# Stick-breaking attention inside a hybrid decoder layer: the float32 work of two heads put side by side

## The chip, the core and the metric

The kernel runs on one core of one Trainium2 chip. The metric is the device time of one execution in microseconds (us), the median of three runs. Lower is better.

## The reference, cut to what matters

The program is one decoder layer: an RMS norm, one input projection into q, k, v (8 heads of 128) and into the channels of a short convolution, stick-breaking attention, the convolution, an output projection and a SwiGLU block. The change concerns the attention alone. For each head, with 528 positions (16 meta tokens and 512 of the sequence) and 128-wide blocks of keys:

```python
z = einsum('bqhd,bkhd->bhqk', q_blk, k_ctx) / sqrt(HEAD_DIM)
causal = kpos[None, :] < qpos[:, None]
log_beta = log_sigmoid(z)
log_keep = where(causal, log_sigmoid(-z), 0.0)
log_pass = cumsum(log_keep, axis=3, reverse=True) - log_keep
w = where(causal, exp(log_beta + log_pass), 0.0)
o = einsum('bhqk,bkhd->bqhd', w, v_ctx)
```

Here z are the logits, w the weights and o the head's output.

## The kernel before

Activations lie transposed: the partitions are channels (or keys), the free dimension is the position. Large products are made of float32r matmuls on values split in two, a high part and a low part (`split`: a cast on ScalarE, a subtraction on VectorE), three matmuls for each pair of tiles. Weights are loaded in pieces of 512 KB, split likewise (lines 203 and 206), and prepared two pieces ahead of the matmuls that use them.

`head(h)` runs three input products for a head, k (`pk`), q (`pq`) and v (`pv`), each over 16 tiles of the contraction ("k tiles"), so 48 k tiles a head. TensorE is kept busy by these products. Attention is cut into steps and put between the k tiles by a counter: `after(n, work)` puts work behind n more k tiles, `tick()` counts each k tile down and runs what is due. A head's attention thus lies in the time of the next head's three products.

Counted from the end of head h's v product (heads 1 to 7), the steps stand like this:

- k tile 6: `turned` turns v with five transposes (lines 626 and 627, float32, into the PSUM tiles `va` and `vb`); VectorE and ScalarE then make `vh`, `vl` and `v32` of it. `attend` follows in the same place. Its logits `z` are in three parts, one for each key block 2, 1, 0 (lines 650 to 652, float32r); the last two key blocks have their own small float32 matmuls, which write the columns 272 to 432 of `z` 2 (lines 648 and 649, "the last logits").
- behind the logits: ScalarE and VectorE make the log terms (lines 673 to 693), with GpSimd for the causal zeros.
- k tile 20 (14 behind `attend`): the running sums of part 2 (`sums`, lines 700 to 703); part 1 six k tiles later, part 0 another six.
- k tile 43 (11 behind part 0): `mix`, the output `o` of 512 columns. Key blocks 0 to 2 are float32r (lines 735 to 737). The last two key blocks are float32: line 738 with 144 columns and line 739 with 16. Then `o` is read by ScalarE (742, and 378 for its squares) and VectorE (743, 379), its stage tile `st_o` is stored (745), and `mix_x(h)` is put behind 742 on ScalarE and behind 743 on VectorE. `mix_x` combines blocks of the input for the convolution (lines 532 to 541): four instructions on ScalarE, six on VectorE, two DMAs.

Head 0 has other counts: transposes at 15, `attend` at 21, sums at 30, 36 and 42, `mix` at 53, which is k tile 5 of the stretch in which head 1's transposes stand at 6. In the same 48 k tiles the next head's own norms are made: `qk_norm` of k puts its sums of squares (lines 555 and 556) 8 k tiles behind the k product, that of q 9 behind the q product.

The pool `sm` has four PSUM tiles of one bank, shared by `va`, `vb`, `z`, `c` (the running sums), `ss_...` (the norms) and `o`. `stage` has two tiles under the tag `st_o`, used by `st_o` and by the two `st_x` of `mix_x`. The order of each engine's queue is laid down before the run by a planner: program order is the priority, `issue_after` forces an order on one engine, `high_priority` lifts an instruction.

After head 7 come the convolution's products. Their inputs are partly read back from DRAM on GpSimd's queue: `mixed` (line 820) and new columns of `n` (line 879).

Of the kernel before, what the change touches and what calls it, by code (L numbers as in the profile page):

```python
# [9 lines left out]
F32 = mybir.dt.float32  # L10
F32R = mybir.dt.float32r
AF = mybir.ActivationFunctionType
ALU = mybir.AluOpType
PSUM = bass.MemoryType.PSUM

P = 128
D = 2048
SEQ = 512
META = 16
L = META + SEQ  # L20
# [6 lines left out]
T2 = SEQ // 2  # L27
EPS = 1e-6

Q0 = [0, 112, 240, 368, 496]  # L30
# [3 lines left out]
def hybrid_layer(ctx: ExitStack, tc: tile.TileContext, xT, w_in, w_out, w_gu, w_down, vecs, out):  # L34
# [10 lines left out]
    ve, sc, gp, pe = nc.vector, nc.scalar, nc.gpsimd, nc.tensor  # L45
# [16 lines left out]
    def t512(cols=SEQ, tag="t", bufs=6):  # L62
        n_tmp[0] += 1
        return tmp.tile([P, cols], F32, tag=tag, bufs=bufs, name=f"tmp{n_tmp[0]}")

    def small(name):
        return sm.tile([P, 512], F32, tag="sm", name=name)
# [6 lines left out]
    g_att, g_cnv = vec[:, 32:40], vec[:, 40:48]  # L74
# [244 lines left out]
    def after(k_tiles, work):  # L319
        waiting.append([k_tiles, work])  # L320
# [33 lines left out]
    def product(parts, acts):  # L354
        for _ in product_steps(parts, acts, len(acts)):
            pass

    def split(hi, lo, src, eng=ve):
        return sc.copy(hi, src), eng.tensor_tensor(lo, src, hi.bitcast(F32), ALU.subtract)  # L359
# [13 lines left out]
    def square_sum(acc, src, first, s=None, eng=gp):  # L373
        if first:
            sc.activation(acc, src, AF.Square)
        else:
            s = t512(src.shape[-1], "r", 3)[:, : src.shape[-1]] if s is None else s
            sc.activation(s, src, AF.Square)
            eng.tensor_tensor(acc, acc, s, ALU.add)
# [56 lines left out]
    def side_by_side(ps):  # L436
        return [(ps[:, 0, :], 0, T2), (ps[:, 1, : L - T2], T2, L)]

    def add_up(ps):
        low = t512(L, "r", 3)[:, :T2]  # L440
        sc.copy(low, ps[:, 0, :T2])
        ve.tensor_tensor(ps[:, 0, T2:], ps[:, 0, T2:], low, ALU.add)

    def two(t):
        return t.rearrange("p (a b) -> p a b", a=2)

    def read_qk(ps, g, cols):

        raw = t512(L, "e", 2)[:, :cols]
        s = t512(L, "e2", 2)[:, :cols]  # L450
        sc.activation(s, ps, AF.Square)
        last = sc.activation(raw, ps, AF.Copy, scale=g)
        return raw, s, cols, last
# [34 lines left out]
    v32 = apool.tile([P, 256], F32, name="v32")  # L488
# [6 lines left out]
    acc_a = accp.tile([P, SEQ], F32, name="acc_a")  # L495
# [19 lines left out]
    oa_dram = [dram.tile([P, 2, SEQ], F32R, name=f"oa_dram{h}") for h in range(HEADS)]  # L515

    def stage(name):
        return stpool.tile([P, 4 * N], F32R, tag="st_o", bufs=2, name=name)
# [9 lines left out]
    def mix_x(k):  # L528

        x = xs[k]  # L530
        for i in range(2):
            sc.activation(x[:, 2 * i : 2 * i + 2], x[:, 2 * i : 2 * i + 2], AF.Copy, scale=g_mix[:, k + 8 * i : k + 8 * i + 1])
        a0, a1, b0, b1 = (x[:, m] for m in range(4))
        ve.tensor_tensor(b1, b1, a1, ALU.subtract)
        ve.tensor_tensor(a1, a0, a1, ALU.subtract)
        ve.scalar_tensor_tensor(a0, b1, -1.0, a0, ALU.mult, ALU.subtract)
        ve.scalar_tensor_tensor(b0, a0, -1.0, b0, ALU.mult, ALU.subtract)
        for m in (2, 0):
            st = stage(f"st_x{k}_{m}").rearrange("p (a b n) -> p a b n", a=2, b=2)
            split(st[:, :, 0], st[:, :, 1], x[:, m : m + 2])  # L540
            gp.dma_start(mix_dram[k // 4][:, 2 - m : 4 - m, k % 4], st.rearrange("p a b n -> p a (b n)"))
# [38 lines left out]
    def head(h):  # L580

        if h:
            pk = pp.tile([P, 2, 512], F32, tag="pp", name=f"pk{h}")
            product(side_by_side(pk), n_hl)
            add_up(pk)
        with tc.issue_after(split_q0[0].ins) if h == 1 else nullcontext():
            read = read_qk(flat(pk), g_k, L) if h else read_k0
        kn = kns[0]
        kh, kl = lent["kh"], lent["kl"]
        after(8 if h else 4, qk_norm(read, kn[:, :L], (kh, kl, 384), f"k{h}"))  # L590

        if h:
            load_mix(h - 1)
            pq = pp.tile([P, 2, 512], F32, tag="pp", name=f"pq{h}")
            product([(pq[:, 0, :], META, L)], n_hl)
        read = read_qk(pq[:, 0, :], gq_s, SEQ) if h else read_q0
        qn, qh, ql = read[0], lent["qh"], lent["ql"]
        after(9 if h else 7, qk_norm(read, None, (qh, ql, SEQ), f"q{h}", ("sh", "sl") if h else ("qh", "ql")))

        pv = pv0  # L600
        if h:
            pv = pp.tile([P, 2, 512], F32, tag="pp", name=f"pv{h}")
            product(side_by_side(pv), n_hl)
            add_up(pv)
        vts = []

        def scale_v():
            vts.append(t512(L, "e", 2) if h else stpool.tile([P, 4 * N], F32, tag="st_o", bufs=2, name="v0"))
            with tc.high_priority(0 if h else 1 << 20):
                ve.tensor_tensor(vts[0][:, :L], flat(pv), r, ALU.mult)  # L610

        if h:
            scale_v()
        else:
            after(2, scale_v)
        if h:
            after(6, lambda: attend(h, kn, kh, kl, qn, qh, ql, turned(h, vts[0])))
        else:
            after(15, lambda: vts.append(turned(h, vts[0])))
            after(21, lambda: attend(h, kn, kh, kl, qn, qh, ql, vts[1]))  # L620

    def turned(h, vt):

        ta, tb = small(f"va{h}"), small(f"vb{h}")
        for b in range(4):
            pe.transpose(ta[:, b * P : (b + 1) * P], vt[:, b * P : (b + 1) * P], ident)
        pe.transpose(tb[:16, :P], vt[:, 512:L], ident)
        vh = apool.tile([P, 384], F32R, tag="vh", name=f"vh{h}")
        vl = apool.tile([P, 384], F32R, tag="vl", name=f"vl{h}")
        with nullcontext() if h else tc.issue_after(split_q0[1].ins):  # L630
            split(vh, vl, ta[:, :384])
            ve.tensor_copy(v32[:16, P:], tb[:16, :P])
            last = ve.tensor_copy(v32[:, :P], ta[:, 384:512])
        if not h:
            behind[0] = last
        return vh, vl

    def attend(h, kn, kh, kl, qn, qh, ql, v):

        vh, vl = v  # L640

        zs = {}
        for b in (2, 1, 0):
            zs[b] = z = small(f"z{h}_{b}")
            kk, q0 = slice(b * P, (b + 1) * P), Q0[b]
            n = SEQ - q0
            if b == 2:
                pe.matmul(z[:, 272:416], kn[:, 384:512], qn[:, 368:], start=True, stop=True)
                pe.matmul(z[:, 416:432], kn[:, 512:640], qn[:, 496:], start=True, stop=True)
            pe.matmul(z[:, :n], kh[:, kk], qh[:, q0:], start=True, stop=False)  # L650
            pe.matmul(z[:, :n], kh[:, kk], ql[:, q0:], start=False, stop=False)
            pe.matmul(z[:, :n], kl[:, kk], qh[:, q0:], start=False, stop=True)


        lw = apool.tile([P, 1344], F32, tag="lw", name=f"lw{h}")
# [14 lines left out]
        for s in (2, 1, 0):  # L670
            a, b = SEG[s]
            z = zs[s][:, : b - a]
# [57 lines left out]
        def mix(ws):  # L730
            o = small(f"o{h}")
            for b in range(3):
                kk, q0 = slice(b * P, (b + 1) * P), Q0[b]
                th, tl = ws[b]
                pe.matmul(o[:, q0:], vh[:, kk], th, start=b == 0, stop=False)
                pe.matmul(o[:, q0:], vh[:, kk], tl, start=False, stop=False)
                pe.matmul(o[:, q0:], vl[:, kk], th, start=False, stop=False)
            pe.matmul(o[:, Q0[3] :], v32[:, :P], lw[:, 1184:1328], start=False, stop=False)
            pe.matmul(o[:, Q0[4] :], v32[:, P:], lw[:, 1328:1344], start=False, stop=True)
            g = g_att[:, h : h + 1]  # L740
            st = stage(f"st_o{h}")[:, : 2 * SEQ].rearrange("p (a b) -> p a b", a=2)
            hi = sc.activation(st[:, 0], o, AF.Copy, scale=g)
            lo = ve.scalar_tensor_tensor(st[:, 1], o, g, st[:, 0].bitcast(F32), ALU.mult, ALU.subtract)
            square_sum(acc_a, o, h == 0, eng=ve)
            gp.dma_start(oa_dram[h], st)
            if h < HEADS - 1:
                with tc.issue_after(hi.ins), tc.issue_after(lo.ins):
                    mix_x(h)

        after(14 if h else 9, lambda: sums(2))  # L750

    for h in range(HEADS):
        head(h)
# [345 lines left out]
    for i, j in enumerate(OUT_TILES):  # L1099
# [83 lines left out]
        else:  # L1183
# [8 lines left out]
            st = two(wide_tmp("st", F32R, 2))  # L1192
# [264 lines left out]
```

## Time and profile before

| what | value |
|---|---|
| time, median of 3 runs | 2020.65 us (2020.52 to 2020.66) |
| profiled execution: its own time | 2020.05 us |
| profiled execution: span, first to last instruction | 2018.3 us |
| TensorE busy | 2013.5 us |
| VectorE / ScalarE / GpSimd busy | 1729.9 / 1080.7 / 337.4 us |

The profile shows one execution. Its own time is 1.75 us more than its span, and 0.6 us less than the median of the runs. Busy time of TensorE is the time in which some matmul was under way; a matmul's record overlaps the next one's, so the distance from start to start tells what one costs.

### The profile page before, as it was taken

The numbers are of one execution on the slowest core, as the hardware profiler recorded it, in microseconds if no ns is written. First come the engines' busy times: TensorE is split into PE (matmuls) and PEld (weight loads), VectorE is DVE, ScalarE is ACT, GpSimd is POOL, SyncE is SP. The second block draws the span as 40 slices with busy tenths as digits, with TensorE's granted clock in tenths as the row PEclk, the third lists the DMA queues.
The fourth block names the chain that finished last, engine by engine and source line by source line (L and its number), as shares of the span: only waits on it lengthen the run. The fifth ranks groups of instructions, "written<-read, shape, count | busy, mean of one in ns | idle before, by whom it ended". The sixth has DMA issues, their size and how long they took to land.

```text
span 2018.3 us, 39281 instructions
## 1 busy us (share of the span) xinstructions
PE 2013.5 (100%) x15934; PEld 1949.8 (97%) x15934; DVE 1729.9 (86%) x2215; ACT 1080.7 (54%) x1574; POOL 337.4 (17%) x508
## 2 busy tenths in 40 slices
PE   9999999999999999999999999999999999999999
PEld 9989999999998889999999999999999999999999
DVE  7887778698888779999998898988988978888888
ACT  7876777354454435555555555555555554444443
POOL 0111111200014430111110110110110333131211
PEclk9999999999999999999999999999999999999999
DMA  6333344823256555565554544554554999797864
GB/s 223 119 133 116 127 140 133 295 95 116 99 203 189 161 155 197 163 176 174 178 155 149 178 152 151 176 155 143 176 160 144 297 342 352 166 324 190 222 150 90
DMA packets 156662, 356.44 MB, mean 177 GB/s; under 512 B 13696, under 2 KB 68224, under 8 KB 155712
## 3 DMA queue, kind: packets, MB, share of 16 engines
q1 hardware_dynamic: 72640, 216.76, 32.6%
q0 software_dynamic: 83696, 137.12, 25.0%
q8 instruction: 125, 2.05, 0.4%
q14 instruction: 57, 0.47, 0.1%
q10 hardware_dynamic: 144, 0.04, 0.0%
HBM read 275.88 MB, written 77.99 MB: 175 GB/s over the span
## 4 chain that ended last, share of the span: by engine, by line
PE 100%; DVE 0%; issue 0%
PE x L909 14%; PE x L913 14%; PE x L912 14%; PE z L909 7%; PE z L912 7%; PE z L913 7%; PE y L909 3%; PE y L912 3%; PE y L913 3%; PE pq L348 3%; PE pk L348 2%; PE pv L348 2%; PE pq L346 1%; PE pv L341 1%; PE pk L341 1%; PE pk L346 1%
## 5 line engine op out<-in xcount | busy, mean ns | idle before, releaser
L203 ACT CAST sw_split<-sw_in 128x1024 fp32r<-128x1024 f32 (+3 forms) x671 | 662.1, 989 | 695.1 <-PE x L912 172.3
L206 DVE TENSOR_TENSOR sw_split<-sw_in,sw_split 128x1024 fp32r<-128x1024 f32 (+3 forms) x671 | 778.0, 1160 | 136.7 <-ACT sw_split L203 128.6
L913 PE MATMUL x<-f,sw_split 128*128 128x256 f32 x1400 | 385.1, 275 | 0.0
L909 PE MATMUL x<-f,sw_split 128*128 128x256 f32 x1400 | 385.1, 275 | 0.0
L912 PE MATMUL x<-f,sw_split 128*128 128x256 f32 x1400 | 385.0, 275 | 0.0
L913 PEld LDWEIGHTS x<-f,sw_split 128*128 128x128 f32 x1400 | 262.8, 188 | 0.2 <-DVE sw_split L206 0.2
L912 PEld LDWEIGHTS x<-f,sw_split 128*128 128x128 f32 x1400 | 262.8, 188 | 0.0
L909 PEld LDWEIGHTS x<-f,sw_split 128*128 128x128 f32 x1400 | 262.8, 188 | 0.0
L1243 POOL DMA_DIRECT2D fd<-s x147 | 103.7, 922 | 706.2 <-DVE s L359 631.9
L909 PE MATMUL z<-f,sw_split 128*128 128x256 f32 x704 | 193.6, 275 | 0.0
L912 PE MATMUL z<-f,sw_split 128*128 128x256 f32 x704 | 193.6, 275 | 0.0
L913 PE MATMUL z<-f,sw_split 128*128 128x256 f32 x704 | 193.6, 275 | 0.0
L216 DVE TENSOR_TENSOR sw_in<-sw_in 128x1024 f32<-128x1024 f32 (+1 forms) x164 | 187.7, 1145 | 5.8 <-DMA sw_in<-w_in 1.0
L909 PE MATMUL x<-ring,sw_split 128*128 128x256 f32 x608 | 167.2, 275 | 0.0
L912 PE MATMUL x<-ring,sw_split 128*128 128x256 f32 x608 | 167.2, 275 | 0.0
L913 PE MATMUL x<-ring,sw_split 128*128 128x256 f32 x608 | 167.2, 275 | 0.0
L909 PEld LDWEIGHTS z<-f,sw_split 128*128 128x128 f32 x704 | 132.1, 188 | 0.0
L912 PEld LDWEIGHTS z<-f,sw_split 128*128 128x128 f32 x704 | 132.1, 188 | 0.0
L913 PEld LDWEIGHTS z<-f,sw_split 128*128 128x128 f32 x704 | 132.1, 188 | 0.0
L909 PEld LDWEIGHTS x<-ring,sw_split 128*128 128x128 f32 x608 | 114.1, 188 | 0.0
L912 PEld LDWEIGHTS x<-ring,sw_split 128*128 128x128 f32 x608 | 114.1, 188 | 0.0
L913 PEld LDWEIGHTS x<-ring,sw_split 128*128 128x128 f32 x608 | 114.1, 188 | 0.0
(730 smaller groups left out, 5271.3 us busy)
## 6 DMA issues: line engine op xcount, KB each, us to landing
sw_in<-w_gu SPq DMA_DIRECT2D x176, 512.0 KB, 3.8
sw_in<-w_in SPq DMA_DIRECT2D x90, 512.0 KB, 3.2
fd<-s POOLq DMA_DIRECT2D x147, 256.0 KB, 4.9
sw_in<-w_down SPq DMA_DIRECT2D x96, 384.0 KB, 4.0
ring<-fd POOLq DMA_DIRECT2D x42, 768.0 KB, 17.9
sw_in<-w_out SPq DMA_DIRECT2D x32, 512.0 KB, 3.3
out_T<-d POOLq DMA_DIRECT2D x54, 256.0 KB, 4.7
mix_dram<-st_x POOLq DMA_DIRECT2D x16, 520.0 KB, 4.0
```

Source lines behind the costliest of these rows:

```text
L203: cast[0] = sc.copy(hi, src)
L206: latest[0] = ve.tensor_tensor(lo, src, hi.bitcast(F32), ALU.subtract)
L216: return ve.tensor_tensor(sums[name], a, b, ALU.add)
L341: pe.matmul(two(ps), wh, n_tiles[k + i][:, :, a:b], start=k + i == 0, stop=k + i == last)
L346: pe.matmul(ps, wh, ah[:, a:b], start=k + i == 0, stop=False)
L348: pe.matmul(ps, w, x[:, a:b], start=False, stop=k + i == last and x is (al if used[0] <= n_first else ah))
L909: opening = pe.matmul(p, hi[:, kk], ah, start=start and j == k == 0, stop=False, skip_group_check=skip)
L912: pe.matmul(p, hi[:, kk], al, start=False, stop=False, skip_group_check=skip)
L913: pe.matmul(p, lo[:, kk], ah, start=False, stop=k == n - 1, skip_group_check=skip)
L1243: gp.dma_start(fd[c][s][:, :, k], t[:, :, i])
```

## The change

The last two output blocks of a head (lines 738 and 739), with all that reads `o` and stores it, are taken out of `mix` and made a function `rest_of_o`. For heads 0 to 6 this runs at the next head's transposes; head 7 runs it at once. At k tile 6, `fp32_group` now runs in this order: `rest_of_o` of the head before, the five transposes, the last logits (648 and 649). The other logits and the rest of `attend` follow four k tiles later, and with them the running sums (24, 30, 36) and `mix` (47). Head 0's own counts stay, but its `rest_of_o` also moves to head 1's group. The fifth transpose of heads 1 to 7 writes into free columns of the tile `pv` in place of `vb`. `mix_x(h)` is no longer forced behind the two reads of `o`.

```diff
+        zs = {}
+        def fp32_group():
+            finish_o.pop()()
+            v = turned(h, vts[0], pv[:, 1, L - T2 :], zs, kn, qn)
+            after(4, lambda: attend(h, kn, kh, kl, qn, qh, ql, v, zs))
         if h:
-            after(6, lambda: attend(h, kn, kh, kl, qn, qh, ql, turned(h, vts[0])))
+            after(6, fp32_group)
...
+    def last_logits(h, zs, kn, qn):
+        zs[2] = z = small(f"z{h}_2")
+        pe.matmul(z[:, 272:416], kn[:, 384:512], qn[:, 368:], start=True, stop=True)
+        pe.matmul(z[:, 416:432], kn[:, 512:640], qn[:, 496:], start=True, stop=True)
+
+    def turned(h, vt, tb=None, zs=None, kn=None, qn=None):
...
+        tb = small(f"vb{h}") if tb is None else tb
...
         pe.transpose(tb[:16, :P], vt[:, 512:L], ident)
+        if h:
+            last_logits(h, zs, kn, qn)
...
-            pe.matmul(o[:, Q0[3] :], v32[:, :P], lw[:, 1184:1328], start=False, stop=False)
-            pe.matmul(o[:, Q0[4] :], v32[:, P:], lw[:, 1328:1344], start=False, stop=True)
-            g = g_att[:, h : h + 1]
-            st = stage(f"st_o{h}")[:, : 2 * SEQ].rearrange("p (a b) -> p a b", a=2)
-            hi = sc.activation(st[:, 0], o, AF.Copy, scale=g)
-            lo = ve.scalar_tensor_tensor(st[:, 1], o, g, st[:, 0].bitcast(F32), ALU.mult, ALU.subtract)
-            square_sum(acc_a, o, h == 0, eng=ve)
-            gp.dma_start(oa_dram[h], st)
             if h < HEADS - 1:
-                with tc.issue_after(hi.ins), tc.issue_after(lo.ins):
-                    mix_x(h)
+                mix_x(h)
+                finish_o.append(lambda: rest_of_o(h, o, lw))
+            else:
+                rest_of_o(h, o, lw)
...
+    def rest_of_o(h, o, lw):
+        pe.matmul(o[:, Q0[3] :], v32[:, :P], lw[:, 1184:1328], start=False, stop=False)
+        pe.matmul(o[:, Q0[4] :], v32[:, P:], lw[:, 1328:1344], start=False, stop=True)
+        g = g_att[:, h : h + 1]
+        st = stage(f"st_o{h}")[:, : 2 * SEQ].rearrange("p (a b) -> p a b", a=2)
+        sc.activation(st[:, 0], o, AF.Copy, scale=g)
+        ve.scalar_tensor_tensor(st[:, 1], o, g, st[:, 0].bitcast(F32), ALU.mult, ALU.subtract)
+        square_sum(acc_a, o, h == 0, eng=ve)
+        gp.dma_start(oa_dram[h], st)
```

## Rows read from the trace of the kernel before

**Rows 1.** The page: span, and busy time of the engines.
```profile
span 2018.3 us, 39281 instructions
...
PE 2013.5 (100%) x15934; PEld 1949.8 (97%) x15934; DVE 1729.9 (86%) x2215; ACT 1080.7 (54%) x1574; POOL 337.4 (17%) x508
```
**Rows 2.** Waits of weight loads (PEld), whole span: us, times, longest; second row.
```profile
PEld pv L346 <- ACT sw_split L203: 0.3, 1, 0.3
```
**Rows 3.** Timeline of PE, heads 0 and 1: start, duration, line, output, shape.
```profile
87.23 0.29 PE L739 MATMUL o<-lw,v 128*128 128x16 f32 x2
87.37 0.37 PE L346 MATMUL pk<-n,sw_split 128*128 128x272 f32 x1
87.58 0.42 PE L348 MATMUL pk<-n,sw_split 128*128 128x272 f32 x2
87.83 0.29 PE L346 MATMUL pk<-n,sw_split 128*128 128x272 f32 x1
...
89.01 0.29 PE L649 MATMUL z<-tmp,kn 128*128 128x16 f32 x2
...
89.36 0.29 PE L651 MATMUL z<-host,host 128*128 128x272 f32 x1
```
**Rows 4.** Timeline of PE, the end of head 1's `mix`.
```profile
121.25 0.29 PE L739 MATMUL o<-lw,v 128*128 128x16 f32 x2
121.39 0.48 PE L341 MATMUL pv<-n,sw_split 128*128 128x512 f32 x1
121.71 0.28 PE L342 MATMUL pv<-n,sw_split 128*128 128x256 f32 x1
121.83 0.39 PE L341 MATMUL pv<-n,sw_split 128*128 128x512 f32 x1
122.06 0.28 PE L342 MATMUL pv<-n,sw_split 128*128 128x256 f32 x1
```
**Rows 5.** Groups by line, 40 to 380 us: weight loads, count, busy us, mean ns.
```profile
L626 PEld LDWEIGHTS va<-ident,tmp 128*128 128x128 f32 x28 | 3.3, 140 | 0.0
...
L739 PEld LDWEIGHTS o<-lw,v 128*128 128x128 f32 x16 | 2.5, 189 | 0.0
```
**Rows 6.** Timeline of VectorE (DVE), 180 to 226 us.
```profile
185.49 0.71 DVE L359 TENSOR_TENSOR host<-tmp,host 128x528 fp32r<-128x528 f32 x1 [0.43 <-ACT host L359]
...
205.48 0.74 DVE L743 SCALAR_TENSOR_TENSOR st_o<-o,vec,st_o 128x512 fp32r<-128x512 f32 x1
...
210.90 0.70 DVE L610 TENSOR_TENSOR tmp<-pv,r 128x528 f32<-128x528 f32 x1
...
222.40 0.69 DVE L359 TENSOR_TENSOR spl<-sp,sph 128x512 fp32r<-128x512 f32 x1 [0.23 <-ACT sph L359]
```
**Rows 7.** Timeline of PE, 180 to 226 us.
```profile
180.54 0.39 PE L346 MATMUL pq<-n,sw_split 128*128 128x512 f32 x1
...
186.68 0.28 PE L555 MATMUL ss_k<-host,ones_r 128*128 128x256 f32 x1
...
211.88 0.60 PE L626 MATMUL va<-ident,tmp 128*128 128x128 f32 x4
...
214.27 0.40 PE L652 MATMUL z<-host,host 128*128 128x512 f32 x1
```
**Rows 8.** Timeline of ScalarE (ACT), 180 to 226 us.
```profile
182.00 0.36 ACT L441 COPY tmp<-pk 128x256 f32<-128x256 f32 x1
...
223.22 0.36 ACT L441 COPY tmp<-pk 128x256 f32<-128x256 f32 x1
```
**Rows 9.** Timeline of GpSimd (POOL), 325 to 405 us, DMA issues.
```profile
369.49 0.54 POOL L745 DMA_DIRECT2D oa_dram<-st_o  x1 [7.80 <-DVE st_o L743]
```
**Rows 10.** Line 879 from 384.5 to 386 us: duration, start; time to landing.
```profile
L879 POOL DMA_DIRECT2D n<-mix_dram x1: 707/707/707, 385.0 to 385.0; - x1
...
DMA to landing us min/median/max: 7.1/7.1/7.1
```
**Rows 11.** Timeline of PE: the first read of the new columns of `n`.
```profile
396.20 0.28 PE L909 MATMUL x<-n,sw_split 128*128 128x260 f32 x1
```

More of the change, by code (lines that the diff above doesn't have):

```diff
@@ L615, in head @@
             after(2, scale_v)
+        zs = {}
[3 more added lines that the diff above has]
+            after(4, lambda: attend(h, kn, kh, kl, qn, qh, ql, v, zs))
         if h:
-            after(6, lambda: attend(h, kn, kh, kl, qn, qh, ql, turned(h, vts[0])))
+            after(6, fp32_group)
         else:
             after(15, lambda: vts.append(turned(h, vts[0])))
-            after(21, lambda: attend(h, kn, kh, kl, qn, qh, ql, vts[1]))
-    def turned(h, vt):
-        ta, tb = small(f"va{h}"), small(f"vb{h}")
+            after(21, lambda: attend(h, kn, kh, kl, qn, qh, ql, vts[1], zs))
+    finish_o = []
+    def last_logits(h, zs, kn, qn):
[3 more added lines that the diff above has]
+    def turned(h, vt, tb=None, zs=None, kn=None, qn=None):
+        ta = small(f"va{h}")
+        tb = small(f"vb{h}") if tb is None else tb
         for b in range(4):
@@ L636, in turned, with attend @@
         return vh, vl
-    def attend(h, kn, kh, kl, qn, qh, ql, v):
+    def attend(h, kn, kh, kl, qn, qh, ql, v, zs):
         vh, vl = v
-        zs = {}
+        if not h:
+            last_logits(h, zs, kn, qn)
         for b in (2, 1, 0):
-            zs[b] = z = small(f"z{h}_{b}")
+            if b < 2:
+                zs[b] = small(f"z{h}_{b}")
+            z = zs[b]
             kk, q0 = slice(b * P, (b + 1) * P), Q0[b]
             n = SEQ - q0
-            if b == 2:
-                pe.matmul(z[:, 272:416], kn[:, 384:512], qn[:, 368:], start=True, stop=True)
-                pe.matmul(z[:, 416:432], kn[:, 512:640], qn[:, 496:], start=True, stop=True)
             pe.matmul(z[:, :n], kh[:, kk], qh[:, q0:], start=True, stop=False)
```

## Prediction

> **What bounds the kernel now.** I read the page first. Matmuls are under way for 2013.5 of the 2018.3 us [rows 1], so only something that shortens or stalls TensorE can move the end. Second came the waits: apart from the start, the longest wait of a weight load is 0.3 us, and it happens once [rows 2]. TensorE is therefore fed all the time, and the other engines matter only where they would make it wait. Third came the timeline of TensorE around the float32 matmuls, to see what they cost from start to start; fourth the timelines of VectorE and ScalarE in one head (180 to 226 us), to see how early each operand is ready; last the stretch behind head 7, where DMAs feed the convolution.
>
> **What a float32 group costs.** In the trace a float32 matmul of line 738 or 739 is two passes. Line 739, with 16 columns, starts at 87.23, and the second matmul of the product behind it starts at 87.58 [rows 3]: 0.35 us for two passes and one float32r matmul. That matmul's ordinary step is 0.125 (87.58 to 87.83 for the two of line 348), so each pass takes 0.11 us, though it has only 16 columns. Behind head 1's `mix` it comes out alike: 121.25 to 121.71 is 0.46, minus 0.23 for a 512-column matmul (121.83 to 122.06), so again 0.11 to 0.12 a pass [rows 4]. And behind the last logits: 89.01 to 89.36 is 0.35 [rows 3]. Such a pass is too short to cover the next matmul's weight load. That shows in the record of the first float32r matmul behind the group: 0.37 us where the next of its kind takes 0.29 [rows 3], or 0.48 where the next takes 0.39 [rows 4]. The engine stands for some 0.08 to 0.09 us at each return from float32 to the products.
>
> **The change, part by part.**
>
> *The junction that goes.* Before, heads 0 to 6 each have two such returns: behind 739 and behind 649. After, 739 is followed by the transposes, and one return is left. Seven go (head 7 still has its own). No matmul is added or dropped, so all that can be saved is this uncovered time. Upper bound: all of it, 7 x 0.09 = 0.63 us. Lower bound: nothing, if the first transpose's weights come no sooner than the product's. I take a value between them: a weight load of the transposes is recorded with 140 ns, one of line 739 with 189 [rows 5], so 0.05 us less stands uncovered: 7 x 0.05 = 0.35 us. The other new junctions, float32r into 738 and 649 into the k product, are of kinds that exist already, and I cost them at nothing.
>
> A rule of the Trainium skill speaks against even this: the page "TensorE: Matmul & The Clock Gate", section "LDWEIGHTS (loading the stationary operand)", lets the load go with the number of columns alone, some 107 ns for 128. The trace agrees for the 16-column passes (0.11 us), but it records the transposes' loads, also of 128 columns, as 49 ns shorter. By the rule the sum would be 0, by the rows 0.35 us.
>
> *The reads of `o`.* Lines 742, 743, 378, 379 and the store move 11 k tiles later. Nothing waits for them soon: `st_o` goes to DRAM. But they hold `o`'s PSUM tile. At k tile 6 the four tiles of `sm` are then `o`, `va`, `z` 2 and, at k tile 10, `z` 1; part 0 of the logits needs `o` or `va` back. Today part 0 needs `va` or `vb` back, and its last matmul starts 2.4 us behind the first transpose (211.88 to 214.27) [rows 7] with no wait. After, that is four k tiles more (0.7 us each: three 512-column matmuls of 0.23), 5.2 us. Reading `o` takes three reads in a row, each like 743's 0.74 us [rows 6], some 2.2 us, on engines that are free of log terms at that point. I cost this at nothing; if it came late, parts 0 and all behind them would wait. On VectorE 743 and 379 stand today ahead of line 610 (210.90 to 211.60), whose result the transposes at 211.88 need [rows 6, 7]. Without them that slack of 0.28 us gets larger.
>
> *Two queues that the store passes.* On GpSimd the store's issue now stands between the causal zeros of two heads; it needs 743, which is read four k tiles before the next log terms begin, so the zeros don't wait for it. And `st_o` now takes its stage tile behind the two `st_x` of its own head: if `mix_x` ran no earlier than its place in program order, k tile 47, their DMAs would have seven k tiles (5 us) to finish before line 742; behind 742 on ScalarE stand the cast to `vh` and a weight cast. Nothing, but it adds to the small-wait rival.
>
> *`mix_x` let loose.* It was held behind 742 and 743; now it is bound only by its loaded x, so the planner may set its ten instructions into any gap of ScalarE and VectorE. They cost TensorE nothing as long as they don't delay an operand (below).
>
> *The fifth transpose into `pv`.* `pv`'s tile is needed again 10 k tiles later by the next q product: some 7 us against a copy that follows at once. Nothing.
>
> *Four k tiles later.* Sums, `mix` and their distances to each other stay as they were, so most operands keep their slack. Two things do not move along. One is the next head's k norm, still at k tile 24 (its split ends at 185.49 + 0.71 = 186.20, its matmul starts at 186.68: slack 0.48 us) [rows 6, 7]. The other is the stretch behind head 7: its store is issued at 369.49 ahead of the loads for the convolution on the same queue, after GpSimd stood 7.80 us for line 743 [rows 9]; this moves by four k tiles, 2.8 us. The last columns of `n` then land, at worst, at 385.0 + 7.1 + 2.8 = 394.9 [rows 10], and TensorE reads them from 396.20 on [rows 11]. They stay hidden, with 1.3 us to spare. If the DMAs run more than that later, TensorE stands for the rest, once.
>
> **Sum.** Against the profiled execution's own 2020.05 us (span 2018.3) it is -0.35, so 2019.7. The median of the runs is 0.6 above that execution; the same -0.35 gives 2020.3 there, which I predict. What a measurement of this kernel can tell from no change is about 0.2%, 4.0 us.
>
> **Rivals.**
>
> *No gain at all:* the transposes' loads are as uncovered as the product's. For it: the pass costs 0.11 us before three different successors. Against it: the recorded lengths of the loads. 2020.65. Chance 0.17.
>
> *A small new wait:* the tail's loads, or single operands, come late by 1 to 2 us in all, because `mix_x` now sits between tighter steps, `st_o` waits for its stage tile, or the loads collide. 2021 to 2022; I take 2021.6. Chance 0.15.
>
> *Slower: the next head's k norm comes late.* A head's period is 41.22 us (line 441 at 182.00 and 223.22) [rows 8], and the k product ends where the q product starts, at 180.54 and so at 221.76 [rows 7]. Before, the log terms thus have 7.1 us between the logits' end (214.27 + 0.40) and the end of the k product, and they end at 222.40 + 0.69 = 223.1 [rows 6], 8.4 us behind the logits. After, the k product's end comes four k tiles sooner relative to them, about 4.3 us behind the logits. So the reading of `pk`, the squares and their split, which are later in program order, meet the log terms on ScalarE and VectorE, with only 0.48 us of slack. From line 441 at 182.00 to the split's end at 186.20 is 4.2 us [rows 6, 8]. Queued wholly behind the log terms, the split would end 8.4 + 4.2 = 12.6 us behind the logits, while the norm's matmul is due about 10 us behind them: 2.6 us late, 18 us over seven heads. Shared out, I put it at 1 us a head: 2020.65 - 0.35 + 7 = 2027.3. It decides from 4.0 / 7 = 0.6 us a head on. For it: both engines are busy there. Against it: there are gaps between the log terms, and the planner may put product matmuls first, so that TensorE need not stand. Chance 0.14.
>
> *Faster by over 4 us:* it would need 0.6 us a head, more than the whole uncovered time that I can see at a return. Chance 0.03.
>
> **Numbers.** The forecast (seven junctions cheaper, no new wait) has 0.48; the rest, 0.03, is unnamed and slower. Faster by over 0.2%: 0.03. Within: 0.48 + 0.17 + 0.15 + 0.01 = 0.81, a small part of the k norm's case lying under the bound. Slower: 0.16. The range reaches from the full 0.63 us and a little scatter, 2019.6, over no gain and the small wait into the beginning of the slower case, 0.4 us a head: 2023.3.
>
> **What would show it.** Right: line 739's second pass is followed by the first transpose within 0.06 to 0.11 us; one long record behind 649 only; a head's period shorter by 0.05 us; no wait in front of lines 555, 650 or 909. Wrong: TensorE waiting for VectorE's split ahead of line 555, for a read of `o` or `va` ahead of part 0 of the logits, or for a DMA ahead of the new columns of `n`; or the period shorter by more than 0.1 us, which would mean that a return from float32 costs more than its first matmul's record shows.

## The result, and the profile after

The changed kernel takes 2030.47 us (median of 6 runs, 2028.61 to 2030.96), the kernel before 2020.61 (6 runs) beside it: a ratio of 1.0047, 95% interval 1.0037 to 1.0057. It is slower by some 10 us, outside the predicted range of 2019.6 to 2023.3. The profiled execution took 2028.61 us, the fastest of the six, so the trace can account for 8.5 us of the 10. Two of the six executions, the profiled one and 2028.90, have a mean granted clock of TensorE of 1.000 of full speed; the other four, 2030.46 to 2030.96, have 0.999.

The page of after, span and busy time [rows 1]:

```profile
span 2026.9 us, 39262 instructions
...
PE 2017.5 (100%) x15934; PEld 1949.9 (96%) x15934; DVE 1731.3 (85%) x2215; ACT 1078.6 (53%) x1574; POOL 343.0 (17%) x508
```

VectorE and ScalarE do the same work as before. The waits of TensorE after, by the line that waits and what it waits for (us in total, times, longest):

```profile
PE c L723 <- DVE spl L359: 2.2, 6, 0.4
PE x L930 <- DMA n<-mix_dram: 1.4, 1, 1.4
...
PE ss_k L555 <- DVE lb L694: 0.5, 1, 0.5
```

And those of its weight loads, whose longest was 0.3 us before, apart from the start [rows 2]:

```profile
PEld c L723 <- DVE spl L359: 3.5, 6, 0.6
PEld x L930 <- DMA n<-mix_dram: 2.1, 3, 1.6
...
PEld ss_k L556 <- DVE host L359: 1.5, 6, 0.3
```

Four places are new: the running sums of part 0 in six heads (line 706 before, 723 now), the norm of k in six heads (line 556), head 0's norm (line 555), and the read of `n` behind head 7 (909 before, 930 now). The first transpose of each head is a good milestone for dating the loss, since the work between two of them is the same before and after:

| first transpose of head | 1 | 2 | 3 | 4 | 5 | 6 | 7 |
|---|---|---|---|---|---|---|---|
| before, us | 88.21 | 129.44 | 170.66 | 211.88 | 253.10 | 294.32 | 335.48 |
| after, us | 89.72 | 131.82 | 173.78 | 215.79 | 257.77 | 299.76 | 341.66 |

So 1.5 us has gone ahead of head 1's transposes, then 6.18 - 1.51 = 4.7 over six heads (0.78 each, the period goes from 41.22 to some 41.98), and nothing from there to the convolution's first product (381.93 before, 388.13 after: 6.2 still). At the first product behind the reads of `n` (399.51 before, 407.99 after) it is 8.5: 2.3 more in the tail.

*The junction that goes.* The timeline of TensorE of after, around the moved float32 matmuls of head 3 in head 4:

```profile
215.65 0.29 PE L765 MATMUL o<-lw,v 128*128 128x16 f32 x2
215.79 0.64 PE L641 MATMUL va<-ident,tmp 128*128 128x128 f32 x4
216.26 0.27 PE L642 MATMUL pv<-ident,tmp 128*16 128x128 f32 x1
...
216.76 0.37 PE L346 MATMUL pk<-n,sw_split 128*128 128x272 f32 x1
```

and before, where a product precedes the transposes, the row that follows the one shown at 211.88 [rows 7]:

```profile
212.31 0.27 PE L627 MATMUL vb<-ident,tmp 128*16 128x128 f32 x1
```

Four transposes take 0.43 us there. After, two passes of line 765 and four transposes take 0.61 (215.65 to 216.26; 0.61 or 0.62 in heads 2 to 7), where the two passes cost 2 x 0.11 = 0.22 before a product [rows 3, 4] and the transposes 0.43: 0.04 to 0.05 us are saved. One long record (0.37) is left, behind 634.

*A steady head.* The timeline of VectorE of after, between the log terms of head 3:

```profile
187.72 0.42 DVE L534 TENSOR_TENSOR x_mix<-x_mix 128x260 f32<-128x260 f32 x1
...
189.61 0.71 DVE L359 TENSOR_TENSOR host<-tmp,host 128x528 fp32r<-128x528 f32 x1
...
195.08 0.69 DVE L359 TENSOR_TENSOR st_x<-x_mix,st_x 128x520 fp32r<-128x520 f32 x1
...
199.95 0.67 DVE L359 TENSOR_TENSOR spl<-lw,sph 1x512 fp32r<-1x512 f32 x1
```

All six of `mix_x`'s VectorE instructions stand there, 3.1 us (four times 0.43, two times 0.69), four of them ahead of the k norm's split (189.61) and all ahead of the split of the carry of part 0 (199.95). TensorE in the same head:

```profile
190.05 0.40 PE L346 MATMUL pq<-n,sw_split 128*128 128x512 f32 x1
190.37 0.51 PE L556 MATMUL ss_k<-host,ones_r 128*128 128x256 f32 x2
190.72 0.63 PE L348 MATMUL pq<-n,sw_split 128*128 128x512 f32 x2
...
199.92 0.41 PE L348 MATMUL pv<-n,sw_split 128*128 128x272 f32 x2
200.67 0.50 PE L723 MATMUL c<-spl,carry 128*128 128x512 f32 x1 [0.34 <-DVE spl L359]
201.01 0.29 PE L346 MATMUL pv<-n,sw_split 128*128 128x272 f32 x1
```

The head's 0.78 can be read off. Two matmuls of 272 columns step 0.25, so line 723 was due at 200.17 and starts 0.50 late. Its own step is 0.34 where a 512-column matmul's is 0.23: 0.11 more. At the norm, line 346 steps 0.32 (0.09 more) and the two of line 556 step 0.35 where two short ones step 0.24 (0.11 more). Together 0.81, less 0.05 of the junction: 0.76.

*The start.* Not all of the 1.5 us belongs to the change: a product of k that starts at 16.77 before starts at 17.20 after, ahead of all of attention. Last_early below, the same program up to head 7, has none of these 0.4 us. From head 0's first float32r logits (58.46 before, 58.90 after) to head 1's transposes it is 29.75 before and 30.82 after: 1.1 us more. In head 0 `mix_x(0)` runs on VectorE from 61.11, the log terms' reads of `z` (lines 693 and 694) behind it, and the norm's second half waits for the tile that they free:

```profile
61.11 0.41 DVE L534 TENSOR_TENSOR x_mix<-x_mix 128x260 f32<-128x260 f32 x1
...
63.52 0.60 DVE L694 SCALAR_TENSOR_TENSOR lb<-z,lw 128x432 f32<-128x432 f32 x1
```

```profile
63.11 0.63 PE L348 MATMUL pq<-n,sw_split 128*128 128x512 f32 x2
64.27 0.36 PE L555 MATMUL ss_k<-host,ones_r 128*128 128x272 f32 x1 [0.53 <-DVE lb L694]
```

Two matmuls of 512 columns step 0.46, and here it is 1.16: 0.7 of the 1.1 us. Of the rest, 0.2 comes at part 1's sums, where line 723 starts only at 73.78 (line 722 at 72.93), and 0.2 in front of head 1's transposes, which wait for line 610.

*The tail.* VectorE, GpSimd and TensorE of after behind head 7 [rows 9 to 11]:

```profile
378.31 1.22 DVE L216 TENSOR_TENSOR sw_in<-sw_in 128x1024 f32<-128x1024 f32 x1 [6.25 <-DMA sw_in<-w_in]
379.45 0.74 DVE L769 SCALAR_TENSOR_TENSOR st_o<-o,vec,st_o 128x512 fp32r<-128x512 f32 x1
```

```profile
380.49 0.54 POOL L771 DMA_DIRECT2D oa_dram<-st_o  x1 [9.94 <-DVE st_o L769]
...
397.84 0.71 POOL L900 DMA_DIRECT2D n<-mix_dram  x1 [1.23 <-DMA mixed<-mix_dram]
```

```profile
406.42 0.39 PE L930 MATMUL x<-n,sw_split 128*128 128x260 f32 x1 [1.37 <-DMA n<-mix_dram]
```

The store is issued 11.0 us later than before (369.49). Of these, 6.2 come from upstream and 2.8 are the four k tiles; some 2 are new: line 769 now stands on VectorE behind a weight's addition (216) that waits for its own DMA. The last load of `n` is issued at 397.84, 12.85 us later than before (384.99).

### The profile page after: what moved, and what is told of

Same layout as the page of the kernel before. It is cut to its first block, busy times and chain, and to the rows that moved or that the text cites. A ratio compares the mean times of both kernels' runs of the same rounds, so it can differ in the third digit from the quotient of the medians.

```text
span 2026.9 us, 39262 instructions
## 1 busy us (share of the span) xinstructions
PE 2017.5 (100%) x15934; PEld 1949.9 (96%) x15934; DVE 1731.3 (85%) x2215; ACT 1078.6 (53%) x1574; POOL 343.0 (17%) x508
## 4 chain that ended last, share of the span: by engine, by line
PE 86%; DVE 4%; issue 4%; ACT 3%; DMA 2%; POOL 1%; SPq 0%; POOLq 0%; DVEq 0%; ACTq 0%
PE x L930 13%; PE x L934 13%; PE x L933 13%; PE z L934 7%; PE z L933 7%; PE z L930 7%; PE y L934 3%; PE y L933 3%; PE y L930 3%; PE pv L348 1%; DVE sw_split L206 1%; PE pv L346 1%; DMA mixed<-mix_dram 1%; PE pk L348 1%; ACT sw_split L203 1%
```

## The experiments

Three theories were held against each other. A: `mix_x`, no longer held, stands between the log terms. B: the four k tiles by themselves make the log terms meet the next head's norm. C: head 7's four k tiles delay the loads behind its store. The first four expectations hold A in its strong form, in which the missing hold costs every head by itself. The kernel before took 2020.3 to 2020.4 us in these comparisons; a period is the distance of the first transposes of one head and the next, from the traces.

| run | what it is | time, us | ratio, interval | period, heads 2 to 6 |
|---|---|---|---|---|
| loose_only | before, `mix_x` not held | 2024.13 | 1.0018 [1.0008, 1.0028] | 41.22 |
| shift_only | before, four k tiles | 2031.14 | 1.0054 [1.0039, 1.0069] | 42.71 |
| no_shift | float32 group moved, no four k tiles | 2024.39 | 1.0022 [1.0012, 1.0032] | 41.41 |
| last_early | after, head 7 at once | 2026.19 | 1.0029 [1.0018, 1.0040] | 41.98 |
| held_at_mix | after, `mix_x` held at `mix` | 2030.34 | 1.0048 [1.0034, 1.0063] | 41.70 |
| both | held_at_mix, head 7 at once | 2030.18 | 1.0050 [1.0035, 1.0065] | 41.69 |
| at_o_last | last_early, `mix_x` behind `o`'s reads | 2024.55 | 1.0018 [1.0009, 1.0028] | 41.26 |
| pv_mix | no four k tiles, `mix_x` behind q's norm | 2024.28 | 1.0019 [1.0010, 1.0028] | 41.3 to 41.9 |
| six_four | at_o_last, heads 6 and 7 as before | 2020.93 | 1.0005 [0.9996, 1.0013] | 41.27 |
| six_two | six_four with two k tiles | 2022.65 | 1.0011 [1.0002, 1.0020] | 41.60 |

**loose_only**, the kernel before with the hold taken off:

```diff
-                with tc.issue_after(hi.ins), tc.issue_after(lo.ins):
-                    mix_x(h)
+                mix_x(h)
```

> The kernel before, with one part of the change alone: mix_x is no longer forced behind the reads of o. Theory A: it is set early here too and meets the same running sums, so the kernel becomes slower by 3 to 6 us, 2024 to 2027, with waits ahead of lines 705 and 706 or 555. Theory B: nothing, 2020.6.

Measured 3.7 us more. In the trace 0.6 of it is there before head 0's logits, 1.7 comes from there to head 1's transposes and 1.5 in head 1; the period stays at 41.22. The two longest waits of TensorE in heads 0 and 1, by its timeline:

```profile
64.45 0.36 PE L555 MATMUL ss_k<-host,ones_r 128*128 128x272 f32 x1 [0.55 <-DVE lb L677]
...
108.05 0.39 PE L556 MATMUL ss_k<-host,ones_r 128*128 128x256 f32 x1 [0.74 <-DVE host L359]
```

The first is head 0's wait as in after, so this loss belongs to the missing hold alone. In steady heads `mix_x`'s additions stand between the log terms here too, and no operand is late: the split of part 0's carry ends at 195.94, and TensorE reads it at 197.05 (1.1 us to spare). So in steady heads the missing hold costs nothing by itself. Nor, as at_o_last shows below, do the four k tiles cost much where `mix_x` is held behind the moved reads of `o`.

**last_early**: head 7's logits at once behind its transposes, all else as after.

```diff
-            after(4, lambda: attend(h, kn, kh, kl, qn, qh, ql, v, zs))
+            rest = lambda: attend(h, kn, kh, kl, qn, qh, ql, v, zs)
+            after(4, rest) if h < HEADS - 1 else rest()
```

> The changed kernel, but head 7's other logits follow its float32 group at once, so that all of its later steps and its store stand four k tiles earlier, as before. Theory C, the store of head 7 delays the loads for the convolution, which TensorE then waits for: the wait ahead of the new columns of n goes, 2.3 to 4 us, to some 2027, the six heads stay at 41.98. If the loads are late for another reason (weights' transfers, the heads' own delay): no change, 2029 to 2030.

It gives back 4.3 us of the median. No wait for `n` is left, and the order on VectorE is that of before, the store's read ahead of the weight's addition:

```profile
374.21 0.75 DVE L770 SCALAR_TENSOR_TENSOR st_o<-o,vec,st_o 128x512 fp32r<-128x512 f32 x1 [2.67 <-ACT st_o L769]
375.98 1.23 DVE L216 TENSOR_TENSOR sw_in<-sw_in 128x1024 f32<-128x1024 f32 x1 [1.02 <-DMA sw_in<-w_in]
```

C is shown: behind head 7 this trace loses 0.1 us in place of 2.3. Of the 4.3 us, 0.4 is the opening of the one trace of after; most of what is left goes with the clock (see Open, below).

**held_at_mix**: after, with `mix_x` held behind the last split of the weights (`mix`, k tile 47).

```diff
-                split(th, tl, w)
+                last_w[:] = split(th, tl, w)
...
-                mix_x(h)
+                with tc.issue_after(last_w[0].ins), tc.issue_after(last_w[1].ins):
+                    mix_x(h)
```

> The changed kernel, with mix_x forced behind the two instructions that split part 0 of the weights (as the kernel before forced it behind the reads of o). Theory A, mix_x let loose was set into the gaps between the running sums and costs 0.78 us a head over six heads and 1.5 us around head 0: the period falls from 41.98 to about 41.17 us, the time by 6.2 us to some 2024, and the loss behind head 7 (2.3 us in the profile) stays. Theory B, the log terms four k tiles later collide with the next head's k norm whatever mix_x does: the period stays near 41.9 and the time near 2029 to 2030.

The time doesn't change, which fits B, but the period is neither theory's. The wait for the carry goes and the period falls to 41.70, but `mix_x` now stands ahead of line 610, and the transposes wait for that. Head 1 pays 3.2 us once (44.89 to the next transposes in place of 41.70): TensorE stands 1.87 us until 107.89, and from 107.8 to 111.4 its granted clock is 0.54, mostly the lower of its two levels (1.2 and 2.4 GHz). The waits of TensorE, the first in head 1, the second at 348.32 in head 7, where part 0 of the logits stands for a read of `o`:

```profile
PE ss_k L555 <- ACT host L359: 1.9, 1, 1.9
PE z L667 <- ACT tmp L378: 1.5, 1, 1.5
...
PE va L641 <- DVE tmp L610: 1.2, 5, 0.3
```

**both**: the edits of held_at_mix and last_early together.

> Both: mix_x forced behind the split of part 0, and head 7's other logits at once. If A and C hold and nothing else is lost, what is left of the change is the dearer junction taken away seven times, 0.39 us by the trace of the changed kernel (two passes of the 16-column matmul take 0.17 instead of 0.225 us): 2020.2. By theory B it stays above 2026.

The two don't add up. The tail's wait goes, and head 7, whose logits now follow at once, stands for a PSUM tile instead, as `o`, `va` and two `z` hold all four of `sm`. The copy that frees `va` (line 651) starts on VectorE at 347.80, behind an instruction of `mix_x` (line 534) that starts after 4.02 us of idle time; ScalarE's part of `mix_x` had stood 5.01 us for its loaded x. The wait:

```profile
PE z L668 <- DVE v L651: 3.0, 1, 3.0
```

**shift_only**: the kernel before with the last logits by the transposes and the others four k tiles later. The float32 matmuls and all reads of `o` stay in `mix`, and `mix_x` stays held behind them.

```diff
-            after(6, lambda: attend(h, kn, kh, kl, qn, qh, ql, turned(h, vts[0])))
+            after(6, fp32_group)
...
+        def fp32_group():
+            v = turned(h, vts[0], pv[:, 1, L - T2 :], zs, kn, qn)
+            after(4, lambda: attend(h, kn, kh, kl, qn, qh, ql, v, zs))
```

> The kernel before, with only the last logits by the transposes and the other logits four k tiles behind them; the float32 matmuls of o stay behind the sums, and mix_x stays held behind the reads of o. Theory A (the late operands come from mix_x's ten operations standing at k tiles 16 to 30, between log terms that now come four k tiles later): mix_x is held until k tile 47 here, so heads 2 to 7 keep a period near 41.25 us, and only the tail's 1.5 to 2.8 us are added: 2022 to 2024. Theory B (the shift alone makes the log terms meet the next head's k norm and split): the period goes to 41.5 to 42.0 us with waits for VectorE in front of the ss_k and c matmuls, and the time to 2025 to 2030.

This is the slowest of all, 1.5 us a head. TensorE waits where neither theory looked, in front of the transposes:

```profile
215.75 0.66 PE L640 MATMUL va<-ident,tmp 128*128 128x128 f32 x4 [1.15 <-DVE tmp L610]
```

and VectorE shows why: the read of `o` (767), its square (379) and two instructions of `mix_x` stand ahead of 442 or 610, four k tiles nearer to the transposes than before.

```profile
211.32 0.75 DVE L767 SCALAR_TENSOR_TENSOR st_o<-o,vec,st_o 128x512 fp32r<-128x512 f32 x1
...
213.38 0.69 DVE L379 TENSOR_TENSOR acc_a<-acc_a,tmp 128x512 f32<-128x512 f32 x1
213.98 0.42 DVE L534 TENSOR_TENSOR x_mix<-x_mix 128x260 f32<-128x260 f32 x1
214.32 0.43 DVE L442 TENSOR_TENSOR pv<-pv,tmp 128x256 f32<-128x256 f32 x1
214.65 0.42 DVE L535 TENSOR_TENSOR x_mix<-x_mix 128x260 f32<-128x260 f32 x1
214.99 0.70 DVE L610 TENSOR_TENSOR tmp<-pv,r 128x528 f32<-128x528 f32 x1
```

So with four k tiles later, the reads of `o` and `mix_x` can't stay where they were; that theory A forecast 41.25 here was wrong, since it looked only at the log terms.

**no_shift**: the float32 group moved, logits at once, `mix_x` held behind the moved reads of `o` (k tile 54).

```diff
+        def fp32_group():
+            finish_o.pop()()
+            v = turned(h, vts[0], pv[:, 1, L - T2 :], zs, kn, qn)
+            attend(h, kn, kh, kl, qn, qh, ql, v, zs)
...
-                with tc.issue_after(hi.ins), tc.issue_after(lo.ins):
-                    mix_x(h)
+                finish_o.append(lambda: rest_of_o(h, o, lw))
...
+        if h < HEADS - 1:
+            with tc.issue_after(hi.ins), tc.issue_after(lo.ins):
+                mix_x(h)
```

> The changed kernel without its four k tiles: the float32 matmuls of o by the transposes and the last logits, the other logits at once behind them, mix_x held behind o's reads at k tile 54. Both theories on the heads (A: loose mix_x, B: the shift) say that the late operands of c and ss_k go. New here: o, va, z 2 and z 1 hold all four PSUM tiles of sm when z 0 wants one, 1.6 us behind the transposes, while the three reads of o take some 2.2 us. I expect TensorE to stand 0.5 to 2 us in front of z 0 in heads 1 to 7, period 41.7 to 43, time 2024 to 2034. If the PSUM tile isn't late, the period is 41.17 and the time 2020.3 to 2022.

The wait for a PSUM tile that was expected never shows. The reads of `o` and `mix_x` stand ahead of the log terms instead, the operands of the sums come late by little (41.41), and in head 7 the cast for the ones (line 719) by 2.2 us:

```profile
PE c L719 <- ACT host L359: 2.2, 1, 2.2
```

**pv_mix**: as no_shift, but all five transposes write `pv`'s tile, and `mix_x` runs early, held behind the reciprocal root of q's norm.

```diff
-            v = turned(h, vts[0], pv[:, 1, L - T2 :], zs, kn, qn)
+            v = turned(h, vts[0], pv, zs, kn, qn)
...
+                with tc.issue_after(q_rsqrt[0].ins), tc.issue_after(q_rsqrt[1].ins):
+                    mix_x(h)
```

> No four k tiles; the float32 matmuls of o by the transposes; all five transposes write pv's tile, so that sm holds o, z 2, z 1 and z 0 and nothing waits for a tile; mix_x stays early (k tile 43) but held behind the q norm's reciprocal root, so that it can't stand between log terms. If the losses of the change come from the shift with the loose mix_x and from nothing in the move of the float32 matmuls, the period is 41.17 (seven times 0.055 us less than before) and the time 2020.0 to 2020.5. A rival: the reads of o now meet the log terms of z 2 on ScalarE and VectorE, or the store passes the queue late, and the c or va operand is late by 0.1 to 0.5 us a head: 2021 to 2024.

The rival holds: no head reaches 41.17, and single operands (the norm's split, the carries) come late by up to 0.8 us.

**at_o_last**: last_early with one difference, `mix_x` held behind the moved reads of `o`, at k tile 54.

```diff
-        sc.activation(st[:, 0], o, AF.Copy, scale=g)
-        ve.scalar_tensor_tensor(st[:, 1], o, g, st[:, 0].bitcast(F32), ALU.mult, ALU.subtract)
+        hi = sc.activation(st[:, 0], o, AF.Copy, scale=g)
+        lo = ve.scalar_tensor_tensor(st[:, 1], o, g, st[:, 0].bitcast(F32), ALU.mult, ALU.subtract)
...
+        if h < HEADS - 1:
+            with tc.issue_after(hi.ins), tc.issue_after(lo.ins):
+                mix_x(h)
```

> The changed kernel with its four k tiles, but mix_x held behind o's reads (as before the change, which is now at k tile 54) and head 7's logits at once. Theory A: with mix_x out of k tiles 16 to 30 and behind the cast of va the period falls to 41.2 to 41.3, and with the tail's loss away the time is 2020.5 to 2022.5. Theory B (the shift alone): the period stays at 41.6 to 42.0 and the time at 2024 to 2027. A point on the side: mix_x's DMAs then start at some 9 us before the next head's reads of the stage tiles, and could themselves be late for the o store: 1 to 2 us once or in each head.

This is the cleanest pair. Against last_early the period falls from 41.98 to 41.26, and the stretch from head 0's first logits to head 1's transposes from 30.84 to 29.65 (29.75 before). On VectorE `mix_x` (from 173.23 on) now ends where the log terms begin, and the carry's split is in time:

```profile
177.66 1.31 DVE L359 TENSOR_TENSOR st_x<-x_mix,st_x 128x520 fp32r<-128x520 f32 x2 [0.46 <-ACT st_x L359]
178.89 0.60 DVE L694 SCALAR_TENSOR_TENSOR sp<-z,lw 128x432 f32<-128x432 f32 x1
...
193.82 0.68 DVE L359 TENSOR_TENSOR spl<-lw,sph 1x512 fp32r<-1x512 f32 x1 [0.42 <-ACT sph L359]
```

It ends at 194.50, and TensorE reads it at 196.60: 2.1 us to spare, where after had none. With the reads of `o` moved and `mix_x` behind them, the four k tiles thus cost the steady heads almost nothing: 41.26 against 41.17 (41.22 less the junction's 0.05) is 0.09 a head. What is left of the time is in head 7: 2.5 us at one wait, by TensorE and then ScalarE,

```profile
352.17 0.50 PE L720 MATMUL c<-host,ones_r 128*128 128x288 f32 x1 [2.01 <-ACT host L359]
```

```profile
351.06 0.73 ACT L532 ACTIVATE x_mix<-x_mix,vec 128x520 f32<-128x520 f32 x1 [1.16 <-DMA x_mix<-xT]
351.70 0.41 ACT L359 CAST host<-lw 128x288 fp32r<-128x288 f32 x1
```

`mix_x(6)` runs so late that the loads for `mix_x(7)` come late too, and the cast for the ones stands on ScalarE behind an instruction that waits for them.

Another 1.6 us follows without any wait. From 352.16 to 355.50 the granted clock is 0.52, mostly its lower level of 1.2 GHz, and a matmul of 260 columns steps 0.22 us (355.08 to 355.30); behind that stretch it steps 0.12 (355.74 to 355.86):

```profile
355.08 0.42 PE L346 MATMUL pu<-n,sw_split 128*128 128x260 f32 x1
355.30 0.60 PE L348 MATMUL pu<-n,sw_split 128*128 128x260 f32 x2
355.74 0.28 PE L346 MATMUL pu<-n,sw_split 128*128 128x260 f32 x1
355.86 0.40 PE L348 MATMUL pu<-n,sw_split 128*128 128x260 f32 x2
```

**six_four** takes that away: head 6's `o` is finished behind its own sums, as before, and six junctions go instead of seven.

```diff
-            finish_o.pop()()
+            if finish_o:
+                finish_o.pop()()
...
-            if h < HEADS - 1:
+            if h < HEADS - 2:
                 finish_o.append(lambda: rest_of_o(h, o, lw))
```

> The run with mix_x behind o's reads at k tile 54, but heads 6 and 7 as before the change: o of head 6 is finished behind its own sums, mix_x of head 6 runs behind its reads, and head 7's logits follow at once. Six junctions go instead of seven. If the 2 us wait for the ones' split in head 7 (and the heads' shift of 0.6 us) are what was left, then the period is 41.25 in heads 2 to 6, 41.2 for head 7, no wait of TensorE over 0.5 us is left and the time is 2020.4 to 2021.2. If mix_x of head 6 still meets head 7's log terms, about 2022.5.

2020.93 us: no difference from before that can be told (0.4 of the 0.8 us between the two traces is there before head 0's logits). Head 7's 41.2 is missed, 42.12, but its transposes only stand behind more products: at 339.68 the trace is 0.7 us behind that of before. Behind the wait of 1.1 us at the very start that before has too, no wait of TensorE is over 0.5 us:

```profile
PE pk L348 <- DVE sw_split L206: 0.5, 1, 0.5
```

**six_two**: the same with `after(2, rest)` in place of `after(4, rest)`.

> The same with two k tiles between the transposes and the logits instead of four. If the shift pushes the log terms against the next head's k norm (0.09 us a head left with four: 41.26 where seven junctions would give 41.17), two k tiles take half of that or all of it: period 41.17 to 41.22, time 2020.0 to 2020.6, as fast as before or a few tenths faster. A rival: o's reads and mix_x now stand ahead of the log terms, as without the four k tiles (41.41): period 41.3 to 41.4, time 2021 to 2022.

The rival holds again: with two k tiles `mix_x` and the reads of `o` delay the sums' operands, and the period is 41.60, more than with none (41.41) or four (41.27). Why two are worse than none stays open.

## Why the prediction was wrong

**What bounds the kernel, and the junction: right.** TensorE was fed all the time before, and its waits after, with the longer steps behind them, are all of the loss that the trace shows but the 0.4 us of the opening. The return that goes saves 0.04 to 0.05 us, as the recorded loads said (0.05). By the rule of the Trainium skill that the prediction weighed ("TensorE: Matmul & The Clock Gate", section "LDWEIGHTS (loading the stationary operand)") it would be nothing; the rows differ, and they decide. Seven of them are 0.3 us, which drown in the rest: no run's steady period fell below the 41.22 of before.

**"The reads of `o`": right, and more than that.** They never hold up a tile in after (in held_at_mix they do, once, in head 7). Shift_only shows that they had to move: left in `mix`, they and the `mix_x` behind them make the transposes wait 1.15 us.

**"`mix_x` let loose ... cost TensorE nothing as long as they don't delay an operand": the step that failed.** The condition was named and then not worked out. Ten instructions, six of them 3.1 us of VectorE, may go into any gap, and in the stretch that the four k tiles tighten they went ahead of the norm's split and of the carry's. It cost 0.78 us a head, 4.7 in six, and 1.1 between head 0's logits and head 1's transposes. Last_early against at_o_last shows both parts by this hold alone (41.98 to 41.26 a head, 30.84 to 29.65 at the start), loose_only that the part at the start needs no shift.

**"Sums, `mix` and their distances to each other stay as they were, so most operands keep their slack": wrong for the carry.** Slack is held against other work on the same engine, too. In loose_only, without the four k tiles, the carry's split had 1.1 us to spare with nearly the same work around it; in after it was 0.34 us late by the wait shown, 0.5 by the start of the matmul.

**The rival of the slower side had the region right, and not the operand.** It put the log terms against the next head's k norm, at 1 us a head. The collision is in that stretch and the size near it, 0.78. Its worst case was a little too large: by its own rows the norm's matmul is due 10.4 us behind the logits (186.68 + 41.22 - 2.8 - 214.67), so 2.2 us late and not 2.6. But the norm's own part is 0.2, the larger one sits in a sum that the rival didn't look at, and the work that decides is `mix_x`, which it left out. Without `mix_x` there, the norm's case gives 0.09 a head (at_o_last), far under the 0.6 from which it would have shown.

**The tail: "They stay hidden, with 1.3 us to spare": wrong.** It moved the store by 2.8 us and kept all else. In the trace the store's read changed places with an addition on VectorE that waited 6.25 us for a weight, and the last load of `n` was issued 12.85 us later, 6.65 beyond the 6.2 from upstream. Last_early, which takes back these four k tiles alone, is 4.3 us faster in the medians. The rival for the tail had put it at 1 to 2 us, together with `mix_x`.

**Open:** the trace of after is 1.9 us faster than its median, and with that goes the mean granted clock, 1.000 against 0.999. Last_early, without the wait for `n`, has 1.000 throughout, and at_o_last shows what such a fall behind a wait costs (1.6 us). That the missing part is a lower clock behind the wait for `n` is therefore likely, but not shown: the one trace of after has 1.000. The traces differ in the opening by up to 0.6 us, for a reason that wasn't followed. And no run has the float32 group moved and `mix_x` loose without the four k tiles, so whether a loose `mix_x` costs a steady head 0.78 us through the four k tiles or through the moved reads of `o` isn't separated.

## What to carry to other kernels

A hold on instructions that nobody waits for isn't idle: it keeps them out of the way of work that somebody does wait for, so before a hold goes, count the released instructions on their engine against the slack of each operand in the stretch that they can reach. When one chain moves against another, look again at everything that was placed by the old distance, including the queue order at the end of the loop. And 0.05 us a head is no reason to touch a schedule in which every head has operands with less than 1 us of slack: here the best repair only came back to where it began.

## What the runs showed of the hardware

A matmul whose weight load waits costs more than its wait. Line 723 waits until 200.67 and then steps 0.34 us where its kind steps 0.23; line 556 steps 0.35 for two where 0.24 is usual, with no wait in TensorE's own list at all. What is late there is the operand of 512 or 256 columns that the matmul reads, not its weights (`carry`, `ones_r`), and still the load is recorded as waiting: that of line 723 starts at 200.67, with the matmul. The 0.1 us is about the uncovered time of a return from float32 (0.08 to 0.09), so a weight load that can't run under the matmul before it seems to leave the same gap, whatever the reason; the runs don't prove that it is the same thing.

A wait can also cost TensorE its clock. Behind 2.01 us of standing in at_o_last the granted clock is 0.52 from 352.16 to 355.50, mostly the lower of its two levels, and 1.6 us more are lost; behind 1.87 us in held_at_mix it is 0.54 (107.8 to 111.4). Behind 2.18 us in no_shift it stays at 1.00 (352 to 358). What decides isn't shown by these runs.
